# A down projection by seven products: six load buffers, loads five steps ahead, another sum for P7, another order of terms, a third plain half

## The chip, the cores and the metric

The kernel runs on one core of a Trainium2 chip. The metric is the device time of one execution in microseconds; the kernel before takes 1382.67 us, the median of three runs (1381.91 to 1382.72). A profile of one execution, taken by the hardware profiler, goes with it. Engines are TensorE (PE; its weight loads are PEld), VectorE (DVE), ScalarE (ACT), GpSimd (POOL) and SyncE (SP), which issues most of the loads here.

## What is computed

One layer of a hybrid decoder block on 512 tokens of width 1024, in float32: a feed-forward half step, a mixer, and a second feed-forward half step.

```python
def swiglu(x, w_gate, w_up, w_down):
    return (jax.nn.silu(x @ w_gate) * (x @ w_up)) @ w_down
...
f = swiglu(rmsnorm(x, ffn1_pre_g[l]), ffn1_w_gate[l], ffn1_w_up[l], ffn1_w_down[l])
x = x + 0.5 * rmsnorm(f, ffn1_post_g[l])
y = hybrid_mixer(rmsnorm(x, mix_pre_g[l]), ...)
x = x + rmsnorm(y, mix_post_g[l])
f = swiglu(rmsnorm(x, ffn2_pre_g[l]), ffn2_w_gate[l], ffn2_w_up[l], ffn2_w_down[l])
x = x + 0.5 * rmsnorm(f, ffn2_post_g[l])
```

The hidden width of a feed-forward step is 2816, which is 22 chunks of 128. The change concerns the last product of `swiglu`, with `w_down`, in both feed-forward steps (their tiles end in `_a` and `_b`).

## The kernel before, in words

**High and low parts.** Every float32 operand of a matmul is split: a rounded high part, made by ScalarE (a cast, `wh`, `xh`), and the rest, made by VectorE as a subtraction (`wl`, `xl`). A product is then three matmuls: high x high, low x high, high x low.

**The down projection** has the activations `aT` (22 chunks of 128 hidden rows, 512 tokens) and the weights `wd` (22 chunks of 128 rows, 1024 columns). Its result, 512 tokens by 1024 columns, fills all eight PSUM banks: four token tiles by two column halves. The class `Down` (from L407) works on the first chunks and then the function `down` (L197), the plain loop, on the rest, chunk by chunk, 24 matmuls each; of its last four chunks the matmuls are held back and done token tile by token tile.

**Seven products for eight.** Chunks 0 to 11 are done in the manner of Strassen and Winograd. Tokens are cut in two halves (i), the 12 chunks in two halves (k), columns in two halves (j). `A(i, k)` and `B(k, j)` are the blocks. Seven products of sums of blocks, P1 to P7, stand in for eight products of blocks. Each is done in three groups g of two chunks, so there are 21 steps, named by product and group: "50" is P5, group 0. Every step is 12 matmuls of 128x512 on two PSUM banks. The sums before a step are VectorE's (`sums`, L436): P5 takes t1 = B01 - B00 and s1 = A10 + A11; P6 takes T2 = B11 - t1, which stays in the tile `T`, and s1 - A00, which stays in `S`; P7 takes B11 - B01 and A00 - A10; P3 takes B11 and A01 - `S`; P4 takes B10 - T2. A load is 512 KB. `LOADS` says which blocks a step loads: P7 loads B11 and B01, and P3 then uses the B11 that P7 loaded.

**Plain halves.** Chunks 12 and 13 (`FILL`) are multiplied plainly, one half of the tokens at a time: p0 and p1 for the first half, q0 and q1 for the second. Each is 12 matmuls too (`step`, L223), each loads its chunk again, and they stand between the products that have more work for VectorE. The plain loop begins at chunk 14.

**The order of the work.** `STEPS` (L400) lists the 25 steps in order. `run` (L519) goes through it: in iteration n it issues the load for step n+3 (`fetch`, L426), VectorE's sums and ScalarE's casts for step n+2, VectorE's low parts for step n+1, and the matmuls of step n (`product`, L485, with the line L497); after some steps `middle` (L500) copies or adds PSUM banks. The first steps are prepared and steps 20 and 21 done while the stage before (gate and up projections, `seven`) still runs. `do` (`Order`, L241) makes VectorE and ScalarE keep this written order, so their operations are shown under L247; loads and matmuls are free for the program's planner, which sets the order of each engine's queue before the kernel runs. On the chip every queue is strictly in its order.

**Buffers.** Loads of the down projection and of the plain weights (`load_w`, L79) share three buffers of 512 KB, tag `wf`. High and low weights have five buffers each, high and low activations too (pool `low_`, set up once the parts of the token sums of the stage before are given up; `self.xp`).

Of the kernel before, what the change touches and what calls it, by code (L numbers as in the profile page):

```python
# [10 lines left out]
F32 = mybir.dt.float32  # L11
# [5 lines left out]
P = 128  # L17
T = 512
# [14 lines left out]
WMAX = 1024  # L33
# [6 lines left out]
def tile_hybrid_block(ctx: ExitStack, tc: tile.TileContext, a: dict):  # L40
    nc = tc.nc
# [5 lines left out]
    act = ctx.enter_context(tc.tile_pool(name="act", bufs=1, side="right"))  # L47
# [17 lines left out]
    def pair(name):  # L65
        return [bank(f"{name}_{b}") for b in range(2)]
# [88 lines left out]
    class PostNorm:  # L155
        def __init__(self, t, g, where, name, half=False):
            self.t, self.g, self.name, self.half = t, g, f"p{name}{t}", half
            self.fg = scratch(f"fg_{name}{t}", *where)
            self.ss = small.tile([P, 2], F32, tag="sp", name=f"sp_{name}{t}")
# [63 lines left out]
    def step(out, xh, xl, wh, wl, t, b, first, last):  # L223
        tk = slice(t * P, (t + 1) * P)
        cs = slice(b * 512, (b + 1) * 512)
        for n, (x, w) in enumerate(((xh, wh), (xl, wh), (xh, wl))):
            nc.tensor.matmul(out, lhsT=x[:, tk], rhs=w[:, cs], start=first and n == 0, stop=last and n == 2,  # L227
                             skip_group_check=True)
# [5 lines left out]
    H = T // 2  # L234
    ADD, SUB, MUL = ALU.add, ALU.subtract, ALU.mult
# [42 lines left out]
    def seven(do, fs, wgu, x, low, scr, aT, name, ahead):  # L278
# [76 lines left out]
        for i in range(len(fs)):  # L355
# [33 lines left out]
            if w:  # L389
# [6 lines left out]
    PLAIN = 4  # L396

    HALF = 6
    FILL = (12, 13)
    STEPS = "20 21 10 50 60 11 51 61 12 52 62 22 p0 p1 70 30 71 31 72 32 40 41 42 q0 q1".split()  # L400
    LOADS = {"1": ((0, 0),), "2": ((1, 0),), "5": ((0, 1),), "6": ((1, 1),), "7": ((1, 1), (0, 1)), "3": (),
             "4": ((1, 0),)}

    def halves(v, n):
        return v.rearrange("p (a b) -> p a b", b=n)

    class Down:  # L407
        after = FILL[-1] + 1

        def __init__(self, do, wdq, wd, aT, scr, name):  # L410
            self.do, self.wdq, self.wd, self.aT, self.scr, self.name = do, wdq, wd, aT, scr, name
            self.xp, self.src, self.x, self.w, self.wf = None, {}, {}, {}, {}
            self.accs = [[None, None] for _ in range(NT)]

        def tt(self, out, p, q, op):
            self.do("vector", "tensor_tensor", out, p, q, op=op)
# [6 lines left out]
        def A(self, i, k, g):  # L423
            return self.aT[:, HALF * k + 2 * g:HALF * k + 2 * g + 2, i * H:(i + 1) * H]

        def fetch(self, s):  # L426
            if s[0] in "pq":
                t = act.tile([P, WMAX], F32, tag="wf", bufs=3, name=f"B{s}_{self.name}")
                nc.sync.dma_start(t, self.wd[FILL[int(s[1])]])
                self.src[s] = self.aT[:, FILL[int(s[1])], None, slice(0, H) if s[0] == "p" else slice(H, T)], halves(t, T)  # L430
            for k, j in LOADS.get(s[0], ()):
                t = act.tile([P, 2, T], F32, tag="wf", bufs=3, name=f"B{k}{j}_{self.name}{s}")
                nc.sync.dma_start(t, halves(self.wdq[int(s[1]), k, j], T))
                self.wf[s[1], k, j] = t

        def sums(self, s, early=False):  # L436
            k, g = s[0], int(s[1])
            if k in "pq":
                return
            A, B = (lambda i, j: self.A(i, j, g)), (lambda i, j: self.wf[s[1], i, j])  # L440
            x = A(*{"1": (0, 0), "2": (0, 1), "4": (1, 1)}.get(k, (0, 0)))
            w = B(*{"1": (0, 0), "2": (1, 0), "3": (1, 1)}[k]) if k in "123" else None
            if k in "64":
                w = self.T[:, 2 * g:2 * g + 2, :]
            if early:
                w = self.scr.tile([P, 2, Q], F32, tag="cd", bufs=1, name=f"t1_{self.name}")
                x = self.scr.tile([P, 2, Q], F32, tag="ab", bufs=1, name=f"s1_{self.name}")[:, :, :H]
            elif k in "57":
                x, w = halves(self.S[:, 7, :], H), self.T[:, 6:8, :]
            if k == "5":  # L450
                self.t1, self.s1 = w, x
                self.tt(w, B(0, 1), B(0, 0), SUB)
                self.tt(x, A(1, 0), A(1, 1), ADD)
            elif k == "6":
                x = halves(self.S[:, g, :], H)
                self.tt(w, B(1, 1), self.t1, SUB)
                self.tt(x, self.s1, A(0, 0), SUB)
            elif k == "7":
                self.tt(w, B(1, 1), B(0, 1), SUB)
                self.tt(x, A(0, 0), A(1, 0), SUB)  # L460
            elif k == "3":
                x = work.tile([P, 2, H], F32, tag="s4", bufs=1, name=f"s4_{self.name}{g}")
                self.tt(x, A(0, 1), halves(self.S[:, g, :], H), SUB)
            elif k == "4":
                self.tt(w, B(1, 0), w, SUB)
            self.src[s] = x, w
# [18 lines left out]
        def product(self, s):  # L485
            k, g = s[0], int(s[1])
            (xh, xl), (wh, wl) = self.x.pop(s), self.w.pop(s)
            if k in "pq":
                for b in range(2):
                    for i in range(2):  # L490
                        step(self.accs[i + 2 * (k == "q")][b], xh[:, i * P:], xl[:, i * P:], wh, wl, 0, b, False, False)
                return
            for i, o in enumerate(self.out[k]):
                for m in range(2):
                    tk, cs = slice(m * H + i * P, m * H + (i + 1) * P), slice(m * T, (m + 1) * T)
                    for n, (x, w) in enumerate(((xh, wh), (xl, wh), (xh, wl))):
                        nc.tensor.matmul(o, lhsT=x[:, tk], rhs=w[:, cs], start=k in "1256" and g + m + n == 0,  # L497
                                         stop=False, skip_group_check=True)

# [19 lines left out]
        def run(self):  # L519
            s0, s1, s2, s3, s4 = STEPS[:5]  # L520
            self.fetch(s0)
            self.sums(s0)
            self.split(s0, "w")
            self.split(s0, "x")
            yield
            self.fetch(s1)
            self.fetch(s2)
            self.fetch(s3)
            self.sums(s1)
            self.split(s1, "w")  # L530
            self.sums(s2)
            self.sums(s3, True)
            yield
            self.split(s1, "x")
            self.split(s2, "w")
            ba, bd, bc, bb = (self.banks(*x) for x in (("a", (0, 1), 0), ("d", (2, 3), 1), ("c", (0, 1), 1),
                                                       ("b", (2, 3), 0)))
            self.out = {"1": bd, "2": ba, "3": bc, "4": bb, "5": bc, "6": bb, "7": bb}
            self.product(s0)
            self.split(s2, "x")  # L540
            self.T = hpool.tile([P, KD, T], F32, tag="hTh", name=f"T_{self.name}")
            self.S = hpool.tile([P, KD, T], F32, tag="hTl", name=f"S_{self.name}")
            self.fetch(s4)
            self.cast(s3, "w")
            yield
            self.cast(s3, "x")
            self.low(s3, "w")
            self.low(s3, "x")
            self.product(s1)
            self.sums(s4)  # L550
            yield
            self.fetch(STEPS[5])
            for x in "wx":
                self.cast(s4, x)
            self.product(s2)
            for n in range(3, len(STEPS)):
                if n + 3 < len(STEPS):
                    self.fetch(STEPS[n + 3])
                if n + 2 < len(STEPS):
                    self.sums(STEPS[n + 2])  # L560
                    for x in "wx":
                        self.cast(STEPS[n + 2], x)
                if n + 1 < len(STEPS):
                    for x in "wx":
                        self.low(STEPS[n + 1], x)
                self.product(STEPS[n])
                self.middle(STEPS[n])
# [557 lines left out]
    for dt in range(KD):  # L1125
# [3 lines left out]
        p2 = pair(f"p2_{dt}")  # L1129
        o = (dt % 2) * 512  # L1130
# [132 lines left out]
```

## Time and profile before

| | |
|---|---|
| median of three runs | 1382.67 us |
| the profiled execution | 1381.4 us |
| its span | 1379.6 us |
| granted TensorE clock, mean | 0.995 |
| ScalarE busy | 600.1 us (43%) |
| moved by DMA | 144.86 MB, 105 GB/s on average |
| first down projection | step 20 starts at 239.57, the plain loop at 322.61 us |
| second down projection | step 20 starts at 1246.88, the plain loop at 1329.44 us |

A row of the order of time has: start, duration (us), engine, line, operation, output tile <- input tiles, shape, count, and in brackets the idle time before it and what ended it. Matmuls are pipelined: a duration of 0.39 us includes the way through the array, and the distance of two starts is what one costs. A row of the waits has: who waited for whom, us in total, times, the longest. A row of the stages has: the stretch, its length, then busy time and count of PE, PEld, DVE, ACT and POOL, the granted clock, the busy share of the DMA engines and GB/s. Tiles named `acca` to `accd` are the four pairs of PSUM banks, `B_a` a load of a block, `Bp_a` and `Bq_a` loads of plain halves, `wf_ad` one of the plain loop, `T_a` and `S_a` VectorE's sums.

### The profile page before, as it was taken

How to read it: one execution, taken by the hardware profiler on the slowest of the kernel's cores; microseconds unless marked ns; L12 is line 12 of the kernel's file. 1: busy time of each engine (PE TensorE's matmuls, PEld its weight loads, DVE VectorE, ACT ScalarE, POOL GpSimd, SP SyncE). 2: the span in 40 equal slices, each digit the busy share in tenths (PEclk: the TensorE clock that was granted, in tenths of full speed). 3: DMA queues.
4: the chain of work that ended last, by engine and by line, in shares of the span. 5: the costliest groups of instructions: out<-in, count | busy, mean ns of one | idle time of the engine just before them, and what ended most of it. 6: DMA issues, size and time to landing. Idle time of an engine off the chain costs nothing.

```text
span 1379.6 us, 19883 instructions
## 1 busy us (share of the span) xinstructions
PE 1353.3 (98%) x7976; PEld 1203.3 (87%) x7976; DVE 967.5 (70%) x1478; ACT 600.1 (43%) x965; POOL 30.1 (2%) x52
## 2 busy tenths in 40 slices
PE   8999999989999999999999999999999999999898
PEld 7899999768899889888888888888888999997676
DVE  7798997976773785675756743333388889888773
ACT  5444444534623632435544543223264444444452
POOL 1000000000200000000000000000010000000000
PEclk9999999999999999999999999999999999999999
DMA  5333333645133222222222232223323233335451
GB/s 200 100 98 109 106 108 99 192 152 169 51 102 127 74 89 80 89 77 77 77 77 79 80 118 77 92 94 105 101 63 97 92 108 102 110 99 176 127 168 61
DMA packets 40540, 144.86 MB, mean 105 GB/s; under 512 B 4620, under 2 KB 4620, under 8 KB 40448
## 3 DMA queue, kind: packets, MB, share of 16 engines
q1 hardware_dynamic: 39312, 140.04, 31.6%
q0 software_dynamic: 1136, 3.56, 0.8%
q8 instruction: 62, 1.02, 0.3%
q14 instruction: 30, 0.25, 0.1%
HBM read 141.48 MB, written 2.10 MB: 104 GB/s over the span
## 4 chain that ended last, share of the span: by engine, by line
PE 90%; DVE 5%; DMA 2%; ACT 1%; issue 1%; POOL 0%; SPq 0%; DVEq 0%; POOLq 0%; ACTq 0%
PE p L176 11%; PE qb_b L319 9%; PE qb_a L319 9%; PE pq L176 7%; PE pm L176 6%; PE qa_b L319 4%; PE qa_a L319 4%; PE pvo L982 2%; PE pvo L984 2%; PE pvo L983 2%; PE acc_o L227 2%; PE pg_a L186 2%; PE pg_b L186 2%; PE pq L186 2%; PE pg_a L176 2%; PE pg_b L176 2%
## 5 line engine op out<-in xcount | busy, mean ns | idle before, releaser
L176 PE MATMUL pq<-hTh_mx,wh_qk 128*128 128x512 f32 x160 | 63.2, 395 | 0.0
L176 PE MATMUL pq<-hTl_mx,wh_qk 128*128 128x512 f32 x160 | 62.4, 390 | 0.0
L88 DVE TENSOR_TENSOR wl_qk<-wf_qk,wh_qk 128x1024 fp32r<-128x1024 f32 x24 | 29.3, 1220 | 41.5 <-ACT wh_qk L86 31.3
L176 PE MATMUL pm<-hTh_mx,wh_mqk 128*128 128x512 f32 x128 | 50.3, 393 | 0.0
L982 PE MATMUL pvo<-wh_vo,hTh_mx 128*128 128x512 f32 x128 | 50.2, 392 | 0.0
L176 PE MATMUL pm<-hTl_mx,wh_mqk 128*128 128x512 f32 x128 | 49.9, 390 | 0.0
L176 PE MATMUL p<-hTh_mx,wh_gm 128*128 128x512 f32 x128 | 49.9, 390 | 0.0
L984 PE MATMUL pvo<-wl_vo,hTh_mx 128*128 128x512 f32 x128 | 49.8, 389 | 0.0
L176 PE MATMUL p<-hTl_mx,wh_gm 128*128 128x512 f32 x128 | 49.8, 389 | 0.0
L983 PE MATMUL pvo<-wh_vo,hTl_mx 128*128 128x512 f32 x128 | 49.8, 389 | 0.0
L86 ACT CAST wh_qk<-wf_qk 128x1024 fp32r<-128x1024 f32 x24 | 25.0, 1045 | 56.2 <-PE pw L730 28.8
L1135 DVE SCALAR_TENSOR_TENSOR t<-t,p 128x512 f32<-128x512 f32 x16 | 11.0, 688 | 42.7 <-PE p L176 42.7
L88 DVE TENSOR_TENSOR wl_mqk<-wf_mqk,wh_mqk 128x1024 fp32r<-128x1024 f32 x16 | 19.6, 1223 | 29.6 <-ACT wh_mqk L86 25.3
L176 PE MATMUL pq<-hTh_mx,wl_qk 128*128 128x512 f32 x160 | 39.6, 389 | 0.0
L873 DVE SCALAR_TENSOR_TENSOR z<-pm,cw,z 128x511 f32<-128x511 f32 (+2 forms) x48 | 35.3, 744 | 1.4 <-ACT z L871 0.9
L319 PE MATMUL qa_a<-hTl_f,wh_a 128*128 128x256 f32 x144 | 36.1, 283 | 0.0
L319 PE MATMUL qa_b<-hTl_f,wh_b 128*128 128x256 f32 x144 | 36.1, 283 | 0.0
L319 PE MATMUL qa_a<-hTh_f,wh_a 128*128 128x256 f32 x144 | 36.1, 283 | 0.0
L319 PE MATMUL qa_b<-hTh_f,wh_b 128*128 128x256 f32 x144 | 36.1, 283 | 0.0
L247 ACT CAST wh_a<-cd_a 128x1024 fp32r<-128x1024 f32 x18 | 18.9, 1051 | 38.9 <-DVE cd_a L247 38.9
L176 PEld LDWEIGHTS pq<-hTh_mx,wl_qk 128*128 128x128 f32 x160 | 30.0, 188 | 6.2
L247 ACT CAST wh_b<-cd_b 128x1024 fp32r<-128x1024 f32 x18 | 18.9, 1051 | 38.0 <-DVE cd_b L247 38.0
(675 smaller groups left out, 4482.5 us busy)
## 6 DMA issues: line engine op xcount, KB each, us to landing
wf_qk<-in_wqk SPq DMA_DIRECT2D x24, 512.0 KB, 3.7
B_a<-in_wdq SPq DMA_DIRECT2D x21, 512.0 KB, 3.7
B_b<-in_wdq SPq DMA_DIRECT2D x21, 512.0 KB, 3.8
g_a<-in_wgu SPq DMA_DIRECT2D x18, 512.0 KB, 3.8
u_a<-in_wgu SPq DMA_DIRECT2D x18, 512.0 KB, 3.8
g_b<-in_wgu SPq DMA_DIRECT2D x18, 512.0 KB, 3.7
u_b<-in_wgu SPq DMA_DIRECT2D x18, 512.0 KB, 3.8
wf_mqk<-in_wmqk SPq DMA_DIRECT2D x16, 512.0 KB, 3.3
```

Of the source, the lines that this page charges most:

```text
L86: nc.scalar.copy(wh, wf)
L88: nc.vector.tensor_tensor(wl, wf, wh.bitcast(F32), op=ALU.subtract)
L176: nc.tensor.matmul(out, lhsT=wt[:, k * P:(k + 1) * P], rhs=x[:, k, tok], start=n == 0, stop=n == len(terms) - 1)
L186: nc.tensor.matmul(outs[b][:, tok], lhsT=ws_[b][w][:, k * P:(k + 1) * P], rhs=x[:, k, tok], start=i + k + hf == 0, stop=hf == 1 and i == 2 ...
L227: nc.tensor.matmul(out, lhsT=x[:, tk], rhs=w[:, cs], start=first and n == 0, stop=last and n == 2, skip_group_check=True)
L247: self.last[eng] = getattr(getattr(nc, eng), fn)(*args, **kw).ins
L319: nc.tensor.matmul(out, lhsT=wt[:, i * P:(i + 1) * P], rhs=y[:, i, :], start=first and n == 0, stop=last and n == len(terms) - 1, skip_gro ...
L873: nc.vector.scalar_tensor_tensor(z[:, s:], src[:, :T - s], cw[:, ct, 3 - s:4 - s], z[:, s:], op0=ALU.mult, op1=ALU.add)
L982: nc.tensor.matmul(out, lhsT=hTh[:, k, tk], rhs=wh[:, cs], start=k == 0, stop=False)
L983: nc.tensor.matmul(out, lhsT=hTl[:, k, tk], rhs=wh[:, cs], start=False, stop=False)
L984: nc.tensor.matmul(out, lhsT=hTh[:, k, tk], rhs=wl[:, cs], start=False, stop=k == KD - 1)
L1135: nc.vector.scalar_tensor_tensor(t1[:, b, :], t1[:, b, :], 1.0, p2[b], op0=ALU.add, op1=ALU.mult)
```

## The change

Five edits, all in `Down`. (1) `room` gives load buffers in turn from the old three and from three new ones (tag `bf`) in the pool `low_`, once that exists; iteration n now fetches step n+5. (2) The loads go through `do`, which keeps them in written order on SP. (3) P7's weight is T2 - B00, which equals B11 - B01; P7 loads B00 alone, and P3 loads B11 itself. (4) In `product` the loop over the three terms is the outermost one: four matmuls high x high, four of xh with wl, four of xl with wh, with the output bank changing at each matmul. (5) `FILL` has chunk 14 as well: p2 stands between 30 and 71, q2 at the end, and the plain loop begins at chunk 15. So there are 27 steps.

```diff
-    FILL = (12, 13)
-    STEPS = "20 21 10 50 60 11 51 61 12 52 62 22 p0 p1 70 30 71 31 72 32 40 41 42 q0 q1".split()
-    LOADS = {"1": ((0, 0),), "2": ((1, 0),), "5": ((0, 1),), "6": ((1, 1),), "7": ((1, 1), (0, 1)), "3": (),
+    FILL = (12, 13, 14)
+    STEPS = "20 21 10 50 60 11 51 61 12 52 62 22 p0 p1 70 30 p2 71 31 72 32 40 41 42 q0 q1 q2".split()
+    LOADS = {"1": ((0, 0),), "2": ((1, 0),), "5": ((0, 1),), "6": ((1, 1),), "7": ((0, 0),), "3": ((1, 1),),
              "4": ((1, 0),)}
...
+        def room(self, n):
+            self.n += 1
+            if self.xp and self.n % 2:
+                return self.xp.tile([P, 2, T], F32, tag="bf", bufs=3, name=n)
+            return act.tile([P, 2, T], F32, tag="wf", bufs=3, name=n)
+
         def fetch(self, s):
             if s[0] in "pq":
-                t = act.tile([P, WMAX], F32, tag="wf", bufs=3, name=f"B{s}_{self.name}")
-                nc.sync.dma_start(t, self.wd[FILL[int(s[1])]])
+                t = self.room(f"B{s}_{self.name}").rearrange("p a b -> p (a b)")
+                self.do("sync", "dma_start", t, self.wd[FILL[int(s[1])]])
...
             for k, j in LOADS.get(s[0], ()):
-                t = act.tile([P, 2, T], F32, tag="wf", bufs=3, name=f"B{k}{j}_{self.name}{s}")
-                nc.sync.dma_start(t, halves(self.wdq[int(s[1]), k, j], T))
+                t = self.room(f"B{k}{j}_{self.name}{s}")
+                self.do("sync", "dma_start", t, halves(self.wdq[int(s[1]), k, j], T))
...
             elif k == "7":
-                self.tt(w, B(1, 1), B(0, 1), SUB)
+                self.tt(w, self.T[:, 2 * g:2 * g + 2, :], B(0, 0), SUB)
...
-            for i, o in enumerate(self.out[k]):
+            for n, (x, w) in enumerate(((xh, wh), (xh, wl), (xl, wh))):
                 for m in range(2):
-                    tk, cs = slice(m * H + i * P, m * H + (i + 1) * P), slice(m * T, (m + 1) * T)
-                    for n, (x, w) in enumerate(((xh, wh), (xl, wh), (xh, wl))):
+                    for i, o in enumerate(self.out[k]):
+                        tk, cs = slice(m * H + i * P, m * H + (i + 1) * P), slice(m * T, (m + 1) * T)
                         nc.tensor.matmul(o, lhsT=x[:, tk], rhs=w[:, cs], start=k in "1256" and g + m + n == 0,
                                          stop=False, skip_group_check=True)
...
             self.product(s2)
+            self.fetch(STEPS[6])
+            self.fetch(STEPS[7])
             for n in range(3, len(STEPS)):
-                if n + 3 < len(STEPS):
-                    self.fetch(STEPS[n + 3])
+                if n + 5 < len(STEPS):
+                    self.fetch(STEPS[n + 5])
```

More of the change, by code (lines that the diff above doesn't have):

```diff
@@ L413, in __init__ @@
             self.accs = [[None, None] for _ in range(NT)]
+            self.n = 0
         def tt(self, out, p, q, op):
```

## The prediction, on record before the result

> **What bounds the kernel now.** I read the page first, then the busy time by stage, then the waits of VectorE, then the order of time on TensorE and on VectorE in the down projection, and last the transfers. The page:
>
> ```profile
> span 1379.6 us, 19883 instructions
> PE 1353.3 (98%) x7976; PEld 1203.3 (87%) x7976; DVE 967.5 (70%) x1478; ACT 600.1 (43%) x965; POOL 30.1 (2%) x52
> ```
>
> TensorE is busy all but 26.3 us of the span, so an edit helps only where TensorE stands or runs slowly. The stages of the first down projection (span, busy time and count of PE, PEld, DVE, ACT, POOL, granted clock, DMA share, GB/s) show where:
>
> ```profile
> 250.00:275.00 25.00, 24.57 (x103) 18.40 (x102) 23.61 (x29) 16.55 (x24) 0.00 (x0) 1.00 0.57 176
> 275.00:300.00 25.00, 19.27 (x73) 14.09 (x72) 17.96 (x23) 9.13 (x12) 0.00 (x0) 0.93 0.42 130
> 300.00:320.00 20.00, 19.29 (x78) 15.27 (x77) 18.91 (x23) 11.08 (x16) 0.00 (x0) 0.92 0.58 182
> 320.00:345.00 25.00, 25.00 (x112) 20.72 (x111) 13.26 (x15) 9.64 (x13) 0.00 (x0) 1.00 0.53 167
> ```
>
> All matmuls there are of one size. The last row, with no idle time, has 112 in 25 us; the second has 73. So TensorE does two thirds of its rate from 275 to 300, VectorE stands 7 us of these 25 as well, and the granted clock falls. VectorE's waits in both projections, one fence each:
>
> ```profile
> DVE T_a L247 <- DMA B_a<-in_wdq: 7.0, 3, 3.3
> ```
>
> ```profile
> DVE T_b L247 <- DMA B_b<-in_wdq: 7.4, 3, 3.6
> ```
>
> Three waits each: the sums of 70, 71 and 72 wait for weights, and TensorE waits for those sums. TensorE in order of time:
>
> ```profile
> 239.57 0.40 PE L497 MATMUL acca_a<-wh_a,xh_a 128*128 128x512 f32 x1
> ...
> 242.32 0.28 PE L319 MATMUL qb_a<-x4h_a,wh_a 128*128 128x256 f32 x1
> ...
> 243.75 0.40 PE L497 MATMUL acca_a<-wh_a,xh_a 128*128 128x512 f32 x1
> ...
> 246.50 0.39 PE L497 MATMUL accd_a<-wh_a,xh_a 128*128 128x512 f32 x1
> ...
> 273.05 0.39 PE L497 MATMUL acca_a<-wh_a,xh_a 128*128 128x512 f32 x1
> ...
> 275.77 0.62 PE L227 MATMUL acca_a<-whp_a,xhp_a 128*128 128x512 f32 x2
> ...
> 279.06 0.61 PE L227 MATMUL accc_a<-whp_a,xhp_a 128*128 128x512 f32 x2
> 282.85 1.22 PE L497 MATMUL accb_a<-wh_a,xh_a 128*128 128x512 f32 x2 [3.17 <-ACT xh_a L247]
> 283.87 0.63 PE L227 MATMUL acca_a<-whp_a,xlp_a 128*128 128x512 f32 x1
> 284.29 0.63 PE L227 MATMUL acca_a<-wlp_a,xhp_a 128*128 128x512 f32 x1
> ...
> 322.61 0.39 PE L227 MATMUL acca_a<-wh_ad,ah_a 128*128 128x512 f32 x1
> ```
>
> The rows are the starts of 20, of a leftover product of the stage before, of 21, of 10, of 22 and of p0; then the second half of p1's high terms, 70's first matmuls after 3.17 us of idle time, p1's low terms behind them; at 322.61 the plain loop begins. Step 22 takes 275.77 - 273.05 = 2.72 us for 12 matmuls, 0.227 us each; right after the idle time they start 0.42 us apart (283.87 to 284.29), so an idle stretch is paid a second time at half rate.
>
> The 25 steps took 322.61 - 239.57 - 1.43 (the leftover product, 242.32 to 243.75) = 81.6 us; at 2.72 us a step the work is 68.0. So 13.6 us are lost. In the second projection:
>
> ```profile
> 1246.88 0.40 PE L497 MATMUL acca_b<-wh_b,xh_b 128*128 128x512 f32 x1
> ...
> 1329.44 0.39 PE L227 MATMUL acca_b<-wh_bd,ah_b 128*128 128x512 f32 x1
> ```
>
> 82.56 - 1.43 = 81.1, so 13.1 are lost. The most that the change can win is 26.7 us. It cannot win all if VectorE has too much to do:
>
> ```profile
> 266.46 1.22 DVE L247 TENSOR_TENSOR wl_a<-T_a,wh_a 128x1024 fp32r<-128x1024 f32 x1
> ...
> 275.06 1.22 DVE L247 TENSOR_TENSOR wlp_a<-Bp_a,whp_a 128x1024 fp32r<-128x1024 f32 x1
> 276.19 0.42 DVE L247 TENSOR_TENSOR xlp_a<-aT_a,xhp_a 128x256 fp32r<-128x256 f32 x1
> 279.92 1.23 DVE L247 TENSOR_TENSOR T_a<-B_a,B_a 128x1024 f32<-128x1024 f32 x1 [3.31 <-DMA B_a<-in_wdq]
> 281.06 0.69 DVE L247 TENSOR_TENSOR S_a<-aT_a 128x512 f32<-128x512 f32 x1
> 281.66 1.22 DVE L247 TENSOR_TENSOR wlp_a<-Bp_a,whp_a 128x1024 fp32r<-128x1024 f32 x1
> 282.80 0.42 DVE L247 TENSOR_TENSOR xlp_a<-aT_a,xhp_a 128x256 fp32r<-128x256 f32 x1
> 283.13 0.69 DVE L247 TENSOR_TENSOR s_a<-aT_a,S_a 128x512 f32<-128x512 f32 x1
> 283.73 1.22 DVE L247 TENSOR_TENSOR wl_a<-T_a,wh_a 128x1024 fp32r<-128x1024 f32 x1
> ```
>
> From start to start an operation on weights (1024) costs 1.14 us, one on activations (512) 0.60, on half of them (256) 0.33. The row with 3.31 us of idle time is the heart of it: 70's sum stands in VectorE's fixed order ahead of p1's low parts, so a late load holds up p1 and 70 alike.
>
> **The change part by part.** *Six buffers, five steps ahead.* In transfers:
>
> ```profile
> B_a<-in_wdq SPq DMA_DIRECT2D x21, 512.0 KB, 3.7
> ```
>
> A load takes 3.7 us to land, 1.4 steps. With six buffers in turn the load of step s waits for the buffer of step s-6, which VectorE has emptied at the latest with the low part of s-6, in iteration s-7. Between that and the first use of s, in iteration s-2, lie four iterations of about 2.7 us, 11 us against 3.7. So all six waits go: 14.4 us on VectorE. The first loads (20, 21, 10, 50, 60, 11) use the old three buffers as before. New buffers stand in room that the parts of the token sums held; their last reader is the leftover product, over at 243.75, before the first such load is wanted; I cost that at nothing, and at 2.7 (one step) each if the room came free a step late.
>
> *Written order.* SP's queue was in order already; a load whose buffer is not free now holds exactly the loads behind it in the list, for which step after step waits. Behind the steps' loads stand the plain loop's own and then the mixer's; chunk 15 is not wanted before q2 is over. By the spacing above no load meets a closed buffer: nothing, at most one landing, 3.7 us.
>
> *P7's weight from T2.* One load for 7 (B00) in place of two, and one for 3 (B11) in place of a buffer held from 7 to 3. VectorE's count stays: one operation on weights, 1.14. The steps' loads stay 25 by this edit; with chunk 14's two they are 27, with one fewer in the plain loop, so one load more in all.
>
> *High terms lead.* The same 12 matmuls; wl is needed 4 matmuls (0.9 us) and xl 8 (1.8 us) after the step's start. What is late next: both output banks now end with the last two matmuls, where 62's sums into PSUM could start after six. VectorE then has four such sums, 2.4 us, and 22 and the first half of p0 (2.72 + 1.36) cover them. Nothing; uncovered, at most 1.4.
>
> *The third plain half.* Chunk 14 leaves the loop (24 matmuls, 5.44 us) and comes as p2 and q2 (2 x 12). TensorE's work is the same. Its weight is split twice: 1.14 more on VectorE, one more copy on ACT (16.55 busy of 25 in the fullest stage). What it buys: from the end of p1's low parts to those of 41, VectorE has 14 operations on weights, 15 on activations (two PSUM sums in it) and a half one: 16.0 + 9.0 + 0.3 = 25.3 us. TensorE has eight matmuls of p1, eight steps and eight matmuls of 41 in that time: 1.8 + 21.8 + 1.8 = 25.4. Even. Without p2 it would be 23.8 against 22.7, so VectorE would hold TensorE 1.1 us. The chunk's old place in the loop needs no cover: VectorE is busy 13.26 of 25 there.
>
> *What remains lost* in each projection. Steps 10 to 62, nine of them, took 273.05 - 246.50 = 26.55 us for 24.5, 2.1 lost with VectorE nearly full (23.61 of 25). Low parts cost VectorE 1.14 + 0.60 = 1.74 a step and the sums of 5 and 6 as much again: 1.74 + 3.48 + 3.48 = 8.70 a trio against TensorE's 8.16, and no load is in that. It ends the wl of 52 (the row at 266.46) at 267.6 after the change too. Without a loss 52 starts at 246.50 + 7 x 2.72 = 265.5 and now wants wl at 266.4: 1.2 lost, between 0 and the 2.1 of before. At p1, 70's sum (1.74) still goes ahead of p1's low parts (1.47): from 276.53 they end at 279.7 to 280.0, its high terms at 278.5 + 0.9 = 279.4: 0.6. At 40 and 41, where the sums of the next weights come in front, 0.6 by the same walk. Sum 2.4, with ends 0 and 4.5 (2.1, and twice the others). Clock: the early stage has small waits and a granted 1.00, so waits of 0.6 should not lower it.
>
> **The sum.** 13.6 - 2.4 = 11.2 and 13.1 - 2.4 = 10.7, together 21.9. The profiled execution took 1381.4 us (span 1379.6 and 1.8 around it), 1.3 under the median of the runs; so 1359.5 for such an execution and 1382.7 - 21.9 = **1360.8** as a median. About 0.2% (2.8 us) is what a measurement can tell from no change.
>
> **The rivals.** *The order on TensorE keeps blocking.* The program's planner sets TensorE's order beforehand: 70's first matmuls stand ahead of p1's low terms at 282.85, and cost p1 its turn. If only VectorE's 14.4 us come back and the rest of the loss stays, 1368.3. Against it: much of the rest is the same waits paid again at half rate.
>
> *The loads stay late*, because a buffer or the room under it comes free late and the written order holds the rest behind it: the 14.4 stay, order and third half give at most the other 7.5: 1375.2. Against it the 11 us of spacing.
>
> *The loads are too slow, and it gets slower.* 27 loads now crowd the steps. If they went one after another at 3.7 us each, the steps would take 99.9 us, where steps and chunk 14 take 81.6 + 5.44 = 87.0 and 86.6 now: 12.9 + 13.3 more, 1408.9. It decides from 3.2 us a load. Against it stand the slices of 3 us from 225 to 345:
>
> ```profile
> GB/s 157 175 0 175 0 205 168 318 243 135 244 254 56 266 213 66 115 161 14 231 119 124 216 10 209 143 206 178 194 130 178 292 195 225 213 279 16 175 5 175
> ```
>
> 318 GB/s is 0.95 MB in 3 us, 1.65 us a load: transfers overlap. The Trainium skill ("DMA: Bandwidth & Descriptors", Bandwidth) says to batch to 1 MiB or more, and has 0.95 us for 64 KB and 6.15 for 1 MB; an estimate between them is 3.4 us for 512 KB, 91 us for 27, and a time of about 1391. By that rule the change loses; the trace's 1.65 disagrees.
>
> *Changing the bank with each matmul*, as the new nesting does, costs. There are 2 x 21 x 12 = 504 such matmuls; 43 ns each would eat the 21.9 us, and half of them at 0.42 for 0.227 would make 1360.8 + 49 = 1410. Against it: p0's high terms go over two banks of both columns at full rate (273.05 to 279.06 is 26 starts at 0.23). The Trainium skill ("TensorE: Matmul & The Clock Gate", A second HAM failure mode) tells of a kernel whose cycling through banks left small idle times that kept lowering the clock; the early stage's 1.00 speaks against it here.
>
> *The time won is lost behind it*: no change, 1382.7. TensorE is full from 320 on with VectorE at half, so nothing there waits for a given hour.
>
> **How the numbers follow.** Forecast 0.72, blocked order 0.14, late loads 0.06, slow loads 0.02, banks 0.03, nothing 0.03. Faster 0.92, the same 0.03, slower 0.05. The forecast's own range is 1356.0 (nothing lost) to 1365.0 (4.5 each); with the blocked order 1356 to 1369, about 8 in 10.
>
> **What would show it.** Right: no waits of T on B in either projection; 239 to the plain loop in about 77.2 us (27 steps, 73.4 + 1.4 + 2.4); granted clock 1.00 in every stage; p1's low terms ahead of 70. Wrong: TensorE waiting for ACT's xh before 70, 71, 72; SP's loads issued less than 4 us before their sums; matmuls over 0.23 us apart in L497 without an idle time; a plain loop that begins with waits for its own weights.

## The result, and the profile after

The changed kernel takes 1359.87 us, the median of four runs (1359.71 to 1361.59); the kernel before took 1382.29 in the runs beside it. The ratio is 0.9843 (95% interval 0.9826 to 0.9860), 22.4 us less. The forecast was 1360.8.

The page of the profiled execution, which with 1361.6 us was the slowest of the four:

```profile
span 1359.8 us, 19896 instructions
PE 1344.6 (99%) x7976; PEld 1202.8 (88%) x7976; DVE 968.4 (71%) x1482; ACT 601.7 (44%) x969; POOL 30.1 (2%) x52
```

TensorE's count is the same; its idle time fell from 26.3 to 15.2 us. The stages of the first down projection, columns as before:

```profile
250.00:275.00 25.00, 24.37 (x106) 19.36 (x105) 23.86 (x29) 16.16 (x23) 0.00 (x0) 1.00 0.66 241
275.00:300.00 25.00, 24.81 (x109) 20.09 (x108) 24.97 (x33) 12.81 (x18) 0.00 (x0) 1.00 0.57 189
300.00:320.00 20.00, 19.74 (x87) 15.84 (x86) 19.30 (x24) 13.71 (x19) 0.00 (x0) 1.00 0.47 148
320.00:345.00 25.00, 25.00 (x112) 20.70 (x111) 12.74 (x18) 8.00 (x15) 0.56 (x1) 1.00 0.41 128
```

From 275 to 300 there are 109 matmuls where there were 73, VectorE is busy 24.97 us of 25 where it stood 7, and the granted clock is 1.00 in every stage where it had been 0.93 and 0.92. The list of VectorE's waits has no row any more in which `T` waits for a load. VectorE in order of time, at the place where it had waited 3.31 us for 70's load:

```profile
268.48 1.22 DVE L247 TENSOR_TENSOR wl_a<-T_a,wh_a 128x1024 fp32r<-128x1024 f32 x1
...
274.32 1.30 DVE L247 TENSOR_TENSOR accb_a<-accb_a,S_a 128x512 f32<-128x512 f32 x2 [0.56 <-PE accb_a L504]
275.53 1.29 DVE L247 TENSOR_TENSOR accc_a<-accb_a,S_a 128x512 f32<-128x512 f32 x2
276.73 1.22 DVE L247 TENSOR_TENSOR wlp_a<-Bp_a,whp_a 128x1024 fp32r<-128x1024 f32 x1
277.86 0.42 DVE L247 TENSOR_TENSOR xlp_a<-aT_a,xhp_a 128x256 fp32r<-128x256 f32 x1
278.19 1.22 DVE L247 TENSOR_TENSOR T_a<-T_a,B_a 128x1024 f32<-128x1024 f32 x1
```

70's sum (now `T_a<-T_a,B_a`, P7's weight from T2) follows p0's low parts at once. TensorE in order of time:

```profile
241.59 1.09 PE L504 MATMUL acca_a<-wh_a,xh_a 128*128 128x512 f32 x4
...
248.52 1.07 PE L504 MATMUL accd_a<-wh_a,xh_a 128*128 128x512 f32 x4
...
274.35 1.07 PE L504 MATMUL acca_a<-wh_a,xh_a 128*128 128x512 f32 x4
...
277.07 0.61 PE L227 MATMUL acca_a<-whp_a,xhp_a 128*128 128x512 f32 x2
277.53 0.61 PE L227 MATMUL accc_a<-whp_a,xhp_a 128*128 128x512 f32 x2
278.33 0.50 PE L227 MATMUL acca_a<-whp_a,xlp_a 128*128 128x512 f32 x1 [0.19 <-DVE xlp_a L247]
...
280.29 0.63 PE L227 MATMUL acca_a<-whp_a,xhp_a 128*128 128x512 f32 x2
...
281.21 0.87 PE L504 MATMUL accb_a<-wh_a,xh_a 128*128 128x512 f32 x3
281.92 0.40 PE L227 MATMUL acca_a<-whp_a,xlp_a 128*128 128x512 f32 x1
...
285.79 1.07 PE L504 MATMUL accc_a<-wh_a,xh_a 128*128 128x512 f32 x4
...
302.11 1.07 PE L504 MATMUL accb_a<-wh_a,xh_a 128*128 128x512 f32 x4
303.44 1.21 PE L504 MATMUL accb_a<-wl_a,xh_a 128*128 128x512 f32 x4 [0.26 <-DVE wl_a L247]
...
305.41 1.08 PE L504 MATMUL accb_a<-wh_a,xh_a 128*128 128x512 f32 x4
...
319.11 0.39 PE L227 MATMUL acca_a<-wh_ad,ah_a 128*128 128x512 f32 x1
```

The rows are the starts of 20, 10, 22, p0 (with its first low term at 278.33), p1, three matmuls of 70 and p1's first low term, then the starts of 30, 40 (with its first wl), 41 and the plain loop. Below, "the steps" of a projection means the time from the start of 20 to that of the plain loop, less the leftover product's 1.43 us; a kernel with 25 steps gets 5.44 us added for chunk 14, so that all do the same work. Here that is 319.11 - 241.59 - 1.43 = 76.1 us, against 81.6 + 5.44 = 87.0 before; in the second projection it is 1315.16 - 1237.59 - 1.43 = 76.1 against 86.6:

```profile
1237.59 1.09 PE L504 MATMUL acca_b<-wh_b,xh_b 128*128 128x512 f32 x4
...
1315.16 0.39 PE L227 MATMUL acca_b<-wh_bd,ah_b 128*128 128x512 f32 x1
```

That is 10.9 + 10.5 = 21.4 us less. The spans differ by 19.8 only, because the profiled execution after lost 2.0 us before the change's place: 20 starts at 241.59 where it had started at 239.57, and the first 60 us, which the change does not touch, had a granted clock of 0.94 in place of 1.00. The two rows, before and after:

```profile
0.00:60.00 60.00, 55.84 (x352) 48.95 (x353) 46.38 (x59) 29.65 (x39) 3.85 (x10) 1.00 0.49 163
```

```profile
0.00:60.00 60.00, 55.21 (x341) 49.53 (x342) 46.12 (x58) 29.71 (x39) 3.84 (x10) 0.94 0.48 158
```

The start of an execution varies by that much in the runs below too (20 starts between 239.6 and 241.6), so small differences are read from the steps, which for most kernels agree to 0.1 us between the two projections, and not from the medians.

### The profile page after: what moved, and what is told of

Read it like the earlier page. It is cut to its first block, busy times and chain, and to the rows that moved or that the text cites. A ratio compares the mean times of both kernels' runs of the same rounds, so it can differ in the third digit from the quotient of the medians.

```text
span 1359.8 us, 19896 instructions
## 1 busy us (share of the span) xinstructions
PE 1344.6 (99%) x7976; PEld 1202.8 (88%) x7976; DVE 968.4 (71%) x1482; ACT 601.7 (44%) x969; POOL 30.1 (2%) x52
## 4 chain that ended last, share of the span: by engine, by line
PE 89%; DVE 6%; ACT 2%; issue 2%; DMA 1%; SPq 0%; DVEq 0%; POOLq 0%; ACTq 0%
PE p L176 11%; PE qb_b L319 9%; PE qb_a L319 9%; PE pq L176 8%; PE pm L176 6%; PE qa_b L319 4%; PE qa_a L319 4%; PE acc_o L227 3%; PE pvo L991 2%; PE pvo L993 2%; PE pvo L992 2%; PE pg_a L186 2%; PE pq L186 2%; PE pg_b L186 2%; PE pg_a L176 2%; PE pg_b L176 2%
```

## The experiments

What was to be told apart: which of the five edits brings the gain; whether depth of loading (my theory) or one load per step does it; and whether the order on TensorE, slow transfers or the change of bank stand in the way. All were timed beside the kernel before, whose median was 1380.2 to 1382.3 us there. The table has the steps of both projections (with chunk 14), the part from 10 to 62 and the part from p0 to 42 of the first (p2 included where there is one), and the time.

| kernel | steps a, b | 10 to 62 | p0 to 42 | median us | ratio to before (95%) |
|---|---|---|---|---|---|
| before | 87.0, 86.6 | 26.55 | 41.40 | 1382.29 | 1 |
| changed | 76.1, 76.1 | 25.83 | 33.88 | 1359.87 | 0.9843 (0.9826 to 0.9860) |
| terms_back | 77.5, 77.5 | 26.50 | 34.61 | 1362.71 | 0.9868 (0.9852 to 0.9885) |
| two_plain | 77.5, 77.5 | 25.87 | 32.56 | 1363.39 | 0.9874 (0.9859 to 0.9889) |
| three_buf | 76.7, 76.5 | 25.85 | 34.46 | 1361.17 | 0.9859 (0.9844 to 0.9873) |
| p7_two_loads | 76.1, 76.1 | 25.85 | 33.91 | 1361.45 | 0.9860 (0.9846 to 0.9875) |
| loads_old | 84.9, 84.9 | 25.88 | 42.62 | 1379.66 | 0.9992 (0.9983 to 1.0001) |
| loads_alone | 78.9, 78.9 | 26.50 | 33.26 | 1365.82 | 0.9892 (0.9878 to 0.9905) |
| t2_alone | 79.5, 78.9 | 26.50 | 33.90 | 1367.06 | 0.9900 (0.9886 to 0.9913) |
| order_free | 76.1, 76.1 | 25.84 | 33.91 | 1359.94 | 0.9850 (0.9836 to 0.9863) |
| loads_twice | 123.7, 121.7 | 40.33 | 60.69 | 1453.28 | 1.0523 (1.0507 to 1.0538) |
| pool_s1 | 76.8, 76.8 | 26.20 | 33.95 | 1361.29 | 0.9859 (0.9845 to 0.9874) |
| bank_last | 75.9, 76.0 | 25.85 | 33.71 | 1360.70 | 0.9852 (0.9836 to 0.9869) |
| more_traffic | 76.1, 76.1 | 25.85 | 33.90 | 1360.43 | 0.9852 (0.9836 to 0.9869) |

**terms_back** has the old nesting of `product` in the changed kernel.

```diff
-            for n, (x, w) in enumerate(((xh, wh), (xh, wl), (xl, wh))):
-                for m in range(2):
-                    for i, o in enumerate(self.out[k]):
+            for i, o in enumerate(self.out[k]):
+                for m in range(2):
+                    for n, (x, w) in enumerate(((xh, wh), (xl, wh), (xh, wl))):
```

> The changed kernel with the nesting of the matmuls of before (bank outermost, then xh wh, xl wh, xh wl for each chunk). Theory (VectorE's low parts are late in the early trios and at 40 and 41, and the new nesting hides 0.9 to 1.8 us of that): 1361.5 to 1364, with 273-to-before's 2.1 us lost again in steps 10 to 62 where the changed kernel loses 1.35, but with 62's sums into PSUM starting earlier, worth 0.4 back at p0. Rival (changing the bank with each matmul costs something): at or under 1359.9. Rival (the planner reorders the matmuls anyway, so the nesting is worth nothing): 1359.9.

Steps 10 to 62 take 26.50 us, as before the change (26.55) and 0.7 more than the changed kernel; p0 to 42 take 0.7 more as well. So the nesting is worth 1.4 us a projection, half of it in the early steps and half behind p0. Behind p0 the two parts of the theory both show: p0 takes 280.59 - 277.75 = 2.84 us, 0.4 less than in the changed kernel (3.2), because 62's sums start earlier, and 40 loses more than that, because TensorE waits for its `xl` with the low terms mixed among the high ones:

```profile
304.36 0.50 PE L504 MATMUL accb_a<-wh_a,xl_a 128*128 128x512 f32 x1 [1.05 <-DVE xl_a L247]
```

The change of bank costs nothing that shows: four matmuls on alternating banks start 0.907 us after the four before them, 0.227 each.

**two_plain** takes p2 and q2 out; chunk 14 is in the plain loop.

```diff
-    FILL = (12, 13, 14)
-    STEPS = "... p0 p1 70 30 p2 71 31 72 32 40 41 42 q0 q1 q2".split()
+    FILL = (12, 13)
+    STEPS = "... p0 p1 70 30 71 31 72 32 40 41 42 q0 q1".split()
```

> The changed kernel without p2 and q2; chunk 14 goes back to the plain loop. Theory (VectorE has 23.8 us of work between p1 and 41 where TensorE has 22.7): 1.1 us more in each projection, 1362.1, seen as waits for low parts at 72 to 41. Rival (the third half only moves work, the loads did it all): 1359.9.

1.4 us more in each projection (1.1 expected). TensorE in order of time has most of it as one wait, at 40:

```profile
301.21 1.21 PE L504 MATMUL accb_a<-wl_a,xh_a 128*128 128x512 f32 x4 [0.98 <-DVE wl_a L247]
```

The row names `wl_a` and not a load, and no wait of VectorE for a load is left in this run: it is VectorE's work and not a late transfer.

**three_buf** has the old buffers and depth, but P7's one load.

```diff
-            if self.xp and self.n % 2:
-                return self.xp.tile([P, 2, T], F32, tag="bf", bufs=3, name=n)
...
-            self.fetch(STEPS[6])
-            self.fetch(STEPS[7])
...
-                if n + 5 < len(STEPS):
-                    self.fetch(STEPS[n + 5])
+                if n + 3 < len(STEPS):
+                    self.fetch(STEPS[n + 3])
```

> The changed kernel with the old three buffers and loads three steps ahead; P7 still loads one block. Theory: the load of step s waits for the low part of s-3 in iteration s-4 and is used in iteration s-2, so two iterations, 5.4 us, stand against 3.7 to 4.9 us of landing: mostly hidden, 1360 to 1366. Rival (depth is what brought the gain): VectorE waits for loads 7 us in each projection again, 1374. Rival (the sum from T2 brought it): 1360.

0.6 and 0.4 us more. The only wait of VectorE for a load that is left in the first projection is 0.37 us, at 72. So six buffers and two more steps of depth are worth half a microsecond when P7 loads one block.

SP's queue shows why one load is enough. In the kernel before, 70's second load was the fourth in a row for three buffers (p0, p1 and the two of 70). It was issued at 276.30, when VectorE had read p0's load (`wlp_a`, 275.06 to 276.28), and 70's sum began at 279.92, as it landed. Here 70's only load takes the third of these buffers, is issued at 271.76, and the sum begins at 276.76 without a wait. The load in the kernel before, then the load and the sum here:

```profile
276.30 0.33 SPq L433 DMA_DIRECT2D B_a<-in_wdq  x1
```

```profile
271.76 0.33 SPq L247 DMA_DIRECT2D B_a<-in_wdq  x1
```

```profile
276.76 1.22 DVE L247 TENSOR_TENSOR T_a<-T_a,B_a 128x1024 f32<-128x1024 f32 x1
```

**p7_two_loads** has P7's old sum with the new buffers.

```diff
-    ... "7": ((0, 0),), "3": ((1, 1),),
+    ... "7": ((1, 1), (0, 1)), "3": (),
...
-                self.tt(w, self.T[:, 2 * g:2 * g + 2, :], B(0, 0), SUB)
+                self.tt(w, B(1, 1), B(0, 1), SUB)
```

> The changed kernel with P7's weight again as B11 - B01, two loads at P7 and none at P3. VectorE's and TensorE's work is the same. Theory: with six buffers five steps ahead even two loads for one step land in time, 1360 to 1362. Rival (one load per step is what brought the gain): VectorE waits for loads at 70, 71, 72 again, up to 1374.

Not one tenth more in the steps. The order on TensorE is the same to the row as in the changed kernel. (Its median is 1.6 us higher; in the profiled executions the last store of the result landed 3.1 us after its issue here and 2.1 in the changed kernel, and that lies behind the steps.) So neither load edit is needed while the other is there; whether either is needed was asked next.

**loads_old** undoes both load edits (the diffs of three_buf and p7_two_loads together).

> The changed kernel with three buffers, three steps ahead and P7's two loads: only the order of terms, the third plain half and the written order stay. Theory now (either of the two load edits is enough, since either alone left only 0 to 0.6 us of a projection's steps undone): without both, VectorE waits again for the loads of 70, 71, 72, and the steps take 5 to 7 us longer in each projection: 1371 to 1375. Rival (high terms and the third half alone give VectorE and TensorE the slack, the loads never mattered): 1361 to 1363.

More was lost than expected: 8.8 us in each projection, and the time is that of the kernel before (0.9992, interval to 1.0001). VectorE's waits and the stage in which they lie:

```profile
DVE T_a L247 <- DMA B_a<-in_wdq: 8.4, 3, 3.4
```

```profile
265.00:290.00 25.00, 21.26 (x79) 16.33 (x78) 19.23 (x25) 12.27 (x19) 0.00 (x0) 0.86 0.47 160
```

The three waits are back, 1.4 us longer in sum than in the kernel before (p2's load now takes one of the same three buffers, which may be the reason; it was not tested), and the lower granted clock is back with them. TensorE's order differs from the changed kernel's in 30 matmuls as well, and what that costs was not measured apart. The new nesting and the third half, worth 2.8 us a projection when loads are in time, save 2.2 and 1.7 of the steps without them. The medians differ by 0.8 only, 3 us less than these 3.9. In the profiled executions 1.1 of that lies ahead of step 20 (it starts at 240.72 where it had started at 239.57) and 1.1 in the last store of the result, which landed 3.1 us after its issue in place of 2.0. The rest is that the profiled execution before, of 1381.4 us, lay 0.9 above the median beside these runs (1380.5).

**loads_alone** is the kernel before with edits (1) and (2) alone; **t2_alone** has edit (3) alone.

> The kernel before with six buffers, five steps ahead and the written order alone; P7 has two loads, the old nesting, no third half. Theory: the steps (25) take 76.1 + 1.4 (old nesting) + 1.4 (no third half) - 5.44 = 73.4 us in each projection, 1365.4 in all, no wait for loads. Rival (the edits help only together): 1372 or more.

> The kernel before with P7's weight from T2, one load at P7 and one at P3, and nothing else. Theory: as with the loads alone and 0.5 us more in each projection, 1366.5. Rival (a late load needs depth as well when the low parts stand right behind it): waits for loads of 7 us in each projection stay in part, 1372 to 1380.

loads_alone has steps of 73.41 and 73.43 us (78.9 with chunk 14) against 73.4 expected; t2_alone has 74.06 and 73.41 against some 73.9. Each edit alone brings most of the gain: 14.7 and 13.4 us of the median. With one of them in place, the nesting and the third half add 1.4 + 1.4 us a projection. In t2_alone what is left of the waits in the first projection is

```profile
DVE T_a L247 <- DMA B_a<-in_wdq: 0.6, 1, 0.6
```

**order_free** issues the loads without `do`. On SP neighbours change places; all other engines have the same order. (The plain loop's first load stands ahead of the last plain half's in the changed kernel too, at 298.21 and 299.34, since `load_w` does not go through `do`.)

```diff
-                self.do("sync", "dma_start", t, self.wd[FILL[int(s[1])]])
+                nc.sync.dma_start(t, self.wd[FILL[int(s[1])]])
...
-                self.do("sync", "dma_start", t, halves(self.wdq[int(s[1]), k, j], T))
+                nc.sync.dma_start(t, halves(self.wdq[int(s[1]), k, j], T))
```

> The changed kernel with loads issued outside the written order: on SP seven pairs of neighbours change places (52 before 12 and the like) and the plain loop's first load comes before the last plain half; the order on every other engine is the same to the row. Theory: with 11 us of spacing a load that comes one place later still lands in time: 1359.9, same. Rival (written order carries part of the gain): 1 to 4 us more, with waits of T or wh for loads.

The same steps to 0.1 us: the written order is worth nothing here.

**loads_twice** issues each load twice into its buffer.

```diff
                 self.do("sync", "dma_start", t, self.wd[FILL[int(s[1])]])
+                self.do("sync", "dma_start", t, self.wd[FILL[int(s[1])]])
...
                 self.do("sync", "dma_start", t, halves(self.wdq[int(s[1]), k, j], T))
+                self.do("sync", "dma_start", t, halves(self.wdq[int(s[1]), k, j], T))
```

> The changed kernel with each of the 27 loads of a projection issued twice into its buffer, one after the other; the second only repeats the first's bytes. It doubles the transfer time of every load. Theory (11 us of spacing against a landing of 4 to 5 us; transfers overlap down to 1.65 us a load): a doubled landing of 8 to 9 us is still inside the spacing, and 54 loads in 76 us are 1.4 us each, near the limit seen: 1360 to 1366. Rival (slow loads: the transfers already fill the steps): each projection's steps take 91 us or more, 1390.

Both expectations were wrong, and the experiment did not measure what it was for. The second load writes the buffer that the first one writes, so it waits on SP's queue until the first has landed, and every later load waits behind it. SP's waits in the first projection say so:

```profile
SPq L247 <- DMA B_a<-in_wdq: 75.5, 18, 6.1
SPq L247 <- DMA Bq_a<-in_wd: 12.3, 3, 5.4
SPq L247 <- DMA Bp_a<-in_wd: 12.0, 3, 4.1
```

It shows the price of a load that blocks the queue, about 4.2 us (99.8 us of waits by 24), not a limit of the transfers.

**more_traffic** was made for that question instead: more bytes, from another queue.

```diff
         def fetch(self, s):
+            if self.xp:
+                t = self.xp.tile([P, T], F32, tag="no", bufs=1, name=f"no{s}_{self.name}")
+                nc.gpsimd.dma_start(t, self.wd[0][:, 0:T])
```

> The changed kernel with 22 more loads of 256 KB in each projection, from GpSimd's queue into a tile that nothing reads; SP's queue is as in the changed kernel. Half as much traffic again, about 270 GB/s through the steps in place of 187. Theory (transfers overlap, and the spacing of 11 us is wide): the steps take the 76.1 us of the changed kernel, up to 77, 1360 to 1361.5, with no wait of T for a load. Rival (slow loads: transfers near their limit at the changed kernel's pace, which the 46 us more a projection of the doubled loads could also mean): waits for loads come back, 10 us or more in each projection, 1380.

Steps of 76.1 us, as in the changed kernel, at 260 GB/s. The stage row of this kernel, and the packets of the changed kernel in the same stretch:

```profile
243.00:319.00 76.00, 74.99 (x329) 60.37 (x329) 73.84 (x90) 45.69 (x64) 10.05 (x19) 1.00 0.75 260
```

```profile
DMA packets 4220, 15.43 MB, mean 203 GB/s; under 512 B 464, under 2 KB 464, under 8 KB 4215
```

The rival of slow transfers falls: a quarter more traffic than the changed kernel's costs nothing. (Half as much again had been reckoned with.)

**pool_s1** moves an activation sum of P5 to GpSimd.

```diff
-                self.tt(x, A(1, 0), A(1, 1), ADD)
+                self.do("gpsimd", "tensor_tensor", x, A(1, 0), A(1, 1), op=ADD)
```

> The changed kernel with the activation sum of P5 (A10 + A11, three per projection) on GpSimd in place of VectorE. Theory (what is left in steps 10 to 62, 25.83 against 24.5 us, is VectorE's 8.70 a trio against TensorE's 8.16): VectorE has 8.10 a trio, these steps take 24.7 to 25.2, 0.6 to 1.1 less in each projection, 1358 to 1359. Rival (GpSimd's sum is slow, or slows VectorE beside it): the cast of 51 and 52 waits for GpSimd, same or slower, 1360 to 1363.

The rival was right: 26.2 us for 10 to 62, 0.4 more. GpSimd's sums, and VectorE's rows beside the second and behind the third:

```profile
231.68 1.30 POOL L247 TENSOR_TENSOR s_a<-aT_a 128x512 f32<-128x512 f32 x1 [213.52 <-DVE wl_a L247]
241.29 1.33 POOL L247 TENSOR_TENSOR S_a<-aT_a 128x512 f32<-128x512 f32 x1 [8.31 <-PE qb_a L319]
...
261.53 6.80 POOL L247 TENSOR_TENSOR S_a<-aT_a 128x512 f32<-128x512 f32 x1 [11.21 <-DVE xl_a L247]
```

```profile
241.38 2.31 DVE L247 TENSOR_TENSOR t_a<-B_a,B_a 128x1024 f32<-128x1024 f32 x1
...
268.36 0.69 DVE L247 TENSOR_TENSOR S_a<-S_a,aT_a 128x512 f32<-128x512 f32 x1 [1.18 <-POOL S_a L247]
```

The second sum started 0.1 us ahead of VectorE's `t_a` and took 1.3 us; `t_a` took 2.31 us, where it takes 1.22 in the changed kernel (241.45). The third started while VectorE was at work without a gap, took 6.8 us, and VectorE then stood 1.18 us until it was done.

**bank_last** ends each step by bank.

```diff
-                for m in range(2):
-                    for i, o in enumerate(self.out[k]):
+                for m, i in ((0, 0), (1, 0), (0, 1), (1, 1)) if n == 2 else ((0, 0), (0, 1), (1, 0), (1, 1)):
+                        o = self.out[k][i]
```

> The changed kernel; only in the last of the three terms the order is by bank, so that the first bank is complete two matmuls before the second instead of one. Theory (p0's loss of about 0.5 us is 62's four sums into PSUM starting late): they start 0.23 us earlier, and p0 loses that much less, 0.2 in each projection, 1359.5; in all else the same. Rival (the change of bank at each matmul costs): the last four of each step would run faster and steps of 2.72 us become shorter, 1355 or less.

As expected: p0 to 42 is 0.2 us shorter. VectorE's row at 62's sums has 0.34 us of idle time where it had 0.56:

```profile
274.13 1.30 DVE L247 TENSOR_TENSOR accb_a<-accb_a,S_a 128x512 f32<-128x512 f32 x2 [0.34 <-PE accb_a L504]
```

In the time it cannot be told from the changed kernel (0.9852 against 0.9843, intervals of 0.0017 either way), so no version here is shown to beat it.

## Why the prediction was right, step by step

- **The loss that could be won** was read as 26.7 us from TensorE's rows, and 21.9 of it forecast. 21.4 came back in the steps; the medians moved by 22.4. Every wait of VectorE for a load went, and the fall of the granted clock with them, as forecast. In the changed kernel 70's load was issued at 266.25 and its sum began at 278.19, 11.9 us later, where the forecast had 11.
- **What remains** was put at 2.4 us a projection and is 76.1 - 73.4 = 2.7. Steps 10 to 62 lose 25.83 - 24.5 = 1.3 (1.2 forecast, from the row of 52's wl alone). At 40 and 41, 302.11 to 305.41 is 3.3 us for 2.72: 0.6, as forecast. Of the rest 0.5 is p0's, which was not forecast, and p1's forecast 0.6 did not come: that the total is so near is in part luck.
- **p0 and p1** were wrong in opposite ways. p1 should have lost 0.6; p1 and 70 take 285.79 - 280.29 = 5.5 us for 5.44, because the planner put three of 70's high matmuls into the gap. The prediction took such a place for a danger, since it had blocked p1 before, and named the opposite order as a sign of being right; here 70's sum was in time, and it blocked nothing. And p0, where I costed 62's late sums into PSUM at nothing, takes 280.29 - 277.07 = 3.2 us: 0.5 lost. It is those sums: started 0.22 us earlier in bank_last, p0 to 42 shortens by 0.2, and with the old nesting in terms_back p0 takes 2.84 us.
- **Six buffers and P7's sum.** This is the step that failed as an explanation, though not in its total. I gave the whole 14.4 us of waits to six buffers and five steps of depth, and costed P7's new sum as changing nothing but loads. Each does the whole work alone: without depth 0.5 us is lost, without the new sum nothing, without both 8.8. The kernel before did not lack depth as such; with three buffers it lacked a place for the second of two loads wanted by one step (issued at 276.30, wanted at 276.6, when p0's low parts were done; the rows at three_buf show it).
- **The third half** was put at 1.1 us a projection and is 1.4; **the nesting** was given 0.9 in the early steps and is 0.7 there, with 0.7 behind p0 that I had not counted.
- **Written order** was costed at nothing and is nothing.
- **The rivals.** Blocked order: the three matmuls of 70 stand ahead of p1's low terms as feared, and cost nothing. Late loads: no wait of VectorE for a load is left. Slow loads: more_traffic rules them out up to 260 GB/s. Change of bank: matmuls still start 0.227 us apart and the granted clock is 1.00 in both down projections. What the Trainium skill ("TensorE: Matmul & The Clock Gate", A second HAM failure mode) tells of cycling through banks does not show here. Time lost behind it: the medians moved by all that the steps won.

That the nesting and the third half save 2.8 us a projection with loads in time and some 2 without goes with the longer waits seen in loads_old (8.4 us against 7.0). The half rate after those waits does not explain it: the granted clock was 0.50 for 6.8 us of the first projection in both (282.67 to 286.08 and 299.74 to 303.15 before, 282.74 to 289.57 in loads_old). Why the saving is smaller stays open.

## What to carry to other kernels

When one stage has several edits, try each alone and each taken away: two of them may be doing the same thing, and then taking one away shows nothing. Add up the work of the engine behind the waiting one per step, in starts and not in durations; here VectorE's 8.70 against TensorE's 8.16 us a trio told to 0.1 us what steps 10 to 62 would still lose when the loads were in time. And where a step wants two loads at once, a formula that reuses a sum already on the chip can be nearly as good as twice the buffers.

## What the runs showed of the hardware

- Of GpSimd and VectorE, the one that was second waited (pool_s1). GpSimd's sum of 128x512 took 1.3 us when it came first, and VectorE's sum of two SBUF inputs that began 0.1 us later took 2.31 us in place of 1.22. Begun while VectorE ran such sums without a gap, GpSimd's took 6.8 us and ended only when VectorE had stood 1.18 us; until then VectorE's operations kept their 0.69 and 1.22 us. The Trainium skill ("SBUF — State Buffer", Who interferes with whom) says that VectorE with two SBUF inputs and a GpSimd operation that reads SBUF share an interface that one of them holds alone; these rows agree.
- Loads of 512 KB from one queue overlap: in the changed kernel two issued at 288.46 and 288.84 landed at 292.77 and 294.00, 1.2 us apart, though each took over 4 us. A quarter more traffic than the changed kernel's, 260 GB/s on average, cost nothing. In loads_twice a load that had to wait for the one before cost about 4.2 us.
- Half rate came back after less idle time than the 3.17 us of the prediction's rows. In the kernel before, TensorE's rows at 72 are

```profile
298.21 0.73 PE L497 MATMUL accb_a<-wh_a,xh_a 128*128 128x512 f32 x2 [1.75 <-ACT xh_a L247]
...
300.03 0.63 PE L497 MATMUL accc_a<-wl_a,xh_a 128*128 128x512 f32 x1
300.46 0.63 PE L497 MATMUL accc_a<-wh_a,xl_a 128*128 128x512 f32 x1
```

  1.75 us without a matmul, and 1.8 us later matmuls start 0.43 us apart. The Trainium skill ("TensorE: Matmul & The Clock Gate", HAM oscillation — how this bites in real kernels) has gaps above some 3.4 us as the danger; here half rate followed a shorter one. One of 1.64 us in the second projection (ahead of 1305.94) was not followed by it; where the limit lies, the runs do not show. The changed kernel's waits of 0.2 to 0.4 us left the granted clock at 1.00.
